# First pair of tiles done plainly, and sums of weights queued behind the layer norm, in the block-product feed-forward parts

## The chip, the cores and the metric

The kernel runs on one core of one Trainium2 chip. The metric is the time of one execution on the device in microseconds; a median of several runs stands for a kernel. TensorE (PE) multiplies, VectorE (DVE) and ScalarE (ACT) do the elementwise work and read products from PSUM, GpSimd (POOL) does some elementwise work in SBUF, and SyncE (SP) issues the transfers.

## What is computed

One step of two hybrid encoder layers over 656 tokens (two request groups side by side), model width 1024, feed-forward width 2816, in float32. Cut to what matters here:

```python
for l in range(2):
    x = post_ln(x, 0.5 * swiglu(x, w_gate[l, 0], w_up[l, 0], w_down[l, 0]))
    x = post_ln(x, mix(l, x))                # even layer: S5 + latent attention; odd layer: attention + retention
    x = post_ln(x, 0.5 * swiglu(x, w_gate[l, 1], w_up[l, 1], w_down[l, 1]))
# swiglu(x, g, u, d) = (silu(x @ g) * (x @ u)) @ d;  post_ln(x, f) = layer_norm(ALPHA * x + f)
```

## The kernel before, in words

Activations lie transposed: features on the partitions, in eight tiles of 128, tokens along the free axis. Each float32 operand of a product is split into a high part `h` (rounded by ScalarE, L286) and a low part `l` (the rest, by VectorE or GpSimd, L289), and each product is three matmuls, h·h, h·l and l·h (`mm3`, `bmm`). `Y3` holds the layer norm's result `y`, `X3` its parts `xh` and `xl`. The norm and the down projection take the tokens in two halves, 336 and 320 columns; the block products take two halves of 328 columns (320 in the last call, where 16 tokens have been dropped).

There are four feed-forward parts. The first (`ffn`) is plain. The other three (`bffn`, for `ff` 1, 2 and 3) form the gate and up products by blocks: a pair of weight tiles times two halves of tokens, with two halves of the contraction, is a 2 x 2 block product, done in seven products P1 to P7 of four contraction tiles each (12 matmuls) where the plain way has eight. P1 and P2 use blocks of the first token half as they are, P3 and P5 blocks of the second half, and P6, P7 and P4 use combinations of blocks, which `combos` makes: differences of `y` in VectorE, then split into `abA` and `abB`. The difference for P5 is written over its block of `xh` and `xl`. On the weight side, `bjob` makes sums and differences of quarter tiles in place in the raw buffers and `ws` (L296 and following), and `bform` splits each result into one of eight half slots of the four pair buffers, in rotation.

At the start of a call, the layer norm of the second half of the tokens is still running. So `bjob_a` first does P1 and P2 for the three pairs of tiles of the first part, gate and up (six jobs of 24 matmuls), which need the first half of the tokens alone; it keeps P1's result in `s1`. The rest of these jobs ("lead jobs") are `bjob` with `s1` given: five products of 12 matmuls each. After the first part come six down tiles' worth of contraction (eight output tiles, `down`), then the second part of the feed-forward width and so on (`SPARTS`: 6, 6, 6 and 4 tiles). The first job of a next part (`ahead`) runs before the down projection of a part, and its last two products among the first down tile.

`layer_norm(h)` runs: sum for the mean on TensorE, differences (VectorE), squares (ScalarE), their sums ending in the "fold" (VectorE), the variance matmul, a reciprocal root of one ScalarE and four VectorE operations (`rsqrt`, L876 to L880), and then `scaled`: a multiplication of two tiles at a time (`ffn_lnt`, VectorE), `xh` on ScalarE (L868), `y` on GpSimd (L869), `xl` on VectorE. With `blocks=True` the first four tiles of the second half get only `y`, on ScalarE (L865), since P5's block is overwritten anyway, and `combos` follows at once.

The order of the instructions on each engine is made by a planner from the order of the program and its own estimate of when each is ready; an instruction written later can go first where an earlier one is not ready. `behind(keys)` ties instructions to named ones of the layer norm (kept in `at`): they stay behind these on that engine. `LN_AFTER` holds such keys for the fetches of `bjob_a` by number; `LN_POOL` names the fetches whose low part is made on GpSimd (0 to 3).

Of the kernel before, what the change touches and what calls it, by code (L numbers as in the profile page):

```python
# [45 lines left out]
LN_AFTER = {1: (("sq", 0, 3),), 2: (("sq", 0, 3),), 3: (("xh", 0, 7), ("y", 0, 7)), 4: (("sq", 1, 3), ("fold", 1, 3))}  # L46
LN_FIRST, LN_FIRST_POOL = LN_AFTER, LN_POOL
# [160 lines left out]
class Prog:  # L208
# [299 lines left out]
    def combos(self):  # L508

        V, w = self.nc.vector, self.wid  # L510
        y = self.Y3
        b11, b12, b21, b22 = (y[:, 4 * i:4 * i + 4, self.cols(j)] for i in range(2) for j in range(2))
# [7 lines left out]
        f = self.forms_x = dict(P1=xb(0, 0), P2=xb(1, 0), P3=xb(1, 1), P5=xb(0, 1), P6=form(at, 0), P7=form(at, 1), P4=form(bt, 0))  # L520
        for c in (0, 2):
            s = slice(c, c + 2)

            def tmp(tag):
                return self.t(tag, [128, 2, 336], F32, 2, self.lnr)[:, :, :w]

            def out(p, d):
                self.split(d, f[p][0][:, s], f[p][1][:, s])
# [5 lines left out]
            out("P6", d2)  # L534
            out("P5", d1)
            d3 = tmp("lnsq")
            self.tt(d3, b22[:, s], b12[:, s], ALU.subtract)
            out("P7", d3)
            d4 = tmp("lnsq")
            V.scalar_tensor_tensor(d4, d2, -1.0, b21[:, s], ALU.mult, ALU.subtract)  # L540
            out("P4", d4)
# [16 lines left out]
    def bconsume(self, gu, q, fi, bank, add, sign):  # L558
# [3 lines left out]
        if gu == 0:  # L562
            if q == (0, 0) and add is None:
# [26 lines left out]

    def bjob_a(self, ff, p, gu, i):

        w = self.job_fetch(self.job(self.I["wgu"][ff, 2 * p, gu], None, None), i, LN_AFTER, LN_POOL)
# [9 lines left out]
    def bjob(self, ff, p, gu, f0, s1=None):  # L603
# [36 lines left out]
        self.tt(s3, a11, a21, ALU.add)  # L640
        self.tt(a21, a21, a22, ALU.add)
        self.tt(a11, a21, a11, ALU.add)
# [19 lines left out]
        self.tt(a12, a11, a12, ALU.add)  # L662
# [5 lines left out]
    def bffn(self, ff, ln_idx, last=False, blocks=False):  # L668
# [46 lines left out]
        for pi, (f0, f1) in enumerate(SPARTS):  # L715
            todo = [(p, gu) for p in range(f0 // 2, f1 // 2) for gu in range(2)]
# [5 lines left out]
            if pi < nparts - 1:  # L722
# [4 lines left out]
                jobs = [down(pi, m) for m in range(8)]  # L727
                for m, j in enumerate(jobs):
# [11 lines left out]
        halves = deque(x[:, :, k:k + 4] for x in self.pairs for k in (0, 4))  # L740
        full, self.pairs = self.pairs, halves
# [14 lines left out]
        self.layer_norm(0, ln_idx, 4.0, last, blocks)  # L756
# [3 lines left out]
        self.layer_norm(1, ln_idx, 4.0, last, blocks)  # L760
        self.pairs = full
# [28 lines left out]
    def mix_out(self, name, ln_idx, h, tick=None, first=True):  # L790

        jobs = [self.out_job(name, m, first) for m in range(8)]
        self.dense_half(jobs, h, {7: lambda: self.layer_norm(h, ln_idx, 1.0, False, True)}, tick)
# [15 lines left out]
    def layer_norm(self, h, idx, epsmul, last, blocks=False):  # L809
# [29 lines left out]
        else:  # L839
            self.scaled(h, idx, last, rs, blocks and h == 1)  # L840
            if blocks and h == 1:
                self.combos()

    def scaled(self, h, idx, last, rs, blocks=False):
# [3 lines left out]
        for m in range(8):  # L848
# [15 lines left out]
            elif blocks and m < 4:  # L864
                at["y", h, m] = nc.scalar.activation(y[:, m], tm, AF.Identity, scale=g[:, m:m + 1], bias=b[:, m:m + 1])  # L865
# [395 lines left out]
    def even_mix(self):  # L1261
# [346 lines left out]
        for hp in range(4):  # L1608
# [4 lines left out]
            for j in range(2):  # L1613
# [18 lines left out]
                   {(h, 7): lambda h=h: self.layer_norm(h, 1, 1.0, False, True) for h in range(2)}, 7)  # L1632
# [488 lines left out]
    def run(self):  # L2121
        tc, nc = self.tc, self.nc
        with tc.tile_pool(name="ps", bufs=1, space=PSUM) as pp, tc.tile_pool(name="dr", bufs=1, space=DRAM) as self.dp:
# [14 lines left out]
            self.bffn(1, 2, blocks=True)  # L2138
# [81 lines left out]
```

## Time and profile before

| | |
|---|---|
| median of 3 runs | 2769.68 us (2768.63 to 2773.45) |
| the profiled execution | 2772.9 us |
| its span, first to last instruction | 2771.1 us |
| mean granted TensorE clock | 0.951 of full speed |
| busy: PE, PEld, DVE, ACT, POOL | 2627.8, 2461.8, 1607.6, 1064.4, 440.4 us |
| matmuls | 17048 |
| moved by the transfers | 243.05 MB |

The profiled execution is 1.8 us longer than its span and 3.2 us longer than the median. A "busy" time is the time in which the engine had at least one instruction running; the busy times of two instructions of one engine overlap a little, since the next starts before the one before has ended. In a timeline a row merges neighbouring instructions of one kind; in brackets stands the engine's idle time before the row and what ended it, and a row without brackets followed without a pause. The granted clock is 1 at 2.4 GHz and 0.5 at 1.2 GHz.

### The profile page before, as it was taken

To read this page: it belongs to the slowest core of one execution; us is meant where nothing else is said; L and a number is where in the kernel's file an instruction comes from. 1 tells how busy PE (TensorE), PEld (TensorE's weight loads), DVE (VectorE), ACT (ScalarE), POOL (GpSimd) and SP (SyncE) were. 2 spreads that over 40 slices of the span, in tenths; PEclk is the share of its full clock that TensorE was granted. 3 is DMA by queue.
4 is the path that set the end of the run, shared out by engine and by line. 5 is a ranking of instruction groups with operands and counts; after the bars stand their busy time and mean duration, and the time that the engine had idled before them with its cause. 6 is when DMAs were issued, how large, how long until landed. Compare 5 with 4: busy or idle time off the path is not lost.

```text
span 2771.1 us, 42830 instructions
## 1 busy us (share of the span) xinstructions
PE 2627.8 (95%) x17048; PEld 2461.8 (89%) x17048; DVE 1607.6 (58%) x2940; ACT 1064.4 (38%) x2010; POOL 440.4 (16%) x557
## 2 busy tenths in 40 slices
PE   9999999999998799999889999989979997999997
PEld 8999999886677799999789999968748996999996
DVE  8343333663436957565895665674323468765756
ACT  3222222434434535343443533343423435443533
POOL 1233311551114000000400000052110023000002
PEclk9999999967998899999989999979979988999998
DMA  4223322342112222222222223222162232322221
GB/s 154 94 87 106 99 93 69 115 126 77 56 41 93 90 84 78 84 80 74 91 79 83 80 81 92 58 64 72 50 204 94 78 126 76 107 77 77 79 86 58
DMA packets 100586, 243.05 MB, mean 88 GB/s; under 512 B 14609, under 2 KB 33186, under 8 KB 100386
## 3 DMA queue, kind: packets, MB, share of 16 engines
q1 hardware_dynamic: 93858, 219.01, 25.2%
q0 software_dynamic: 6528, 21.30, 2.5%
q8 instruction: 134, 2.20, 0.3%
q14 instruction: 66, 0.54, 0.1%
HBM read 221.92 MB, written 17.14 MB: 86 GB/s over the span
## 4 chain that ended last, share of the span: by engine, by line
PE 88%; DVE 6%; ACT 2%; issue 2%; DMA 1%; POOL 1%; SPq 0%; DVEq 0%; ACTq 0%; POOLq 0%
PE psum L267 58%; PE psum L549 27%; PE psum L270 2%; DVE ffn_lnt L296 1%; POOL keep_y L869 1%; DVE ffn_lnva L296 1%; DVE ffn_sg L296 1%; DVE keep_x L289 1%; DVE ring_pair L289 1%; ACT ring_pair L286 1%; DVE keep_y L296 0%; DMA even_in_raw<-uv 0%; DVE ring_raw L296 0%; DVE abA L289 0%; DMA ring_raw<-wdn 0%
## 5 line engine op out<-in xcount | busy, mean ns | idle before, releaser
L286 ACT ACTIVATE ring_pair<-ring_raw 128x512 fp32r<-128x512 f32 (+3 forms) x607 | 448.7, 742 | 824.6 <-PE psum L267 498.6
L267 PE MATMUL psum<-keep_x,ring_pair 128*128 128x320 f32 (+2 forms) x4272 | 700.6, 322 | 31.1 <-ACT ring_pair L286 7.6
L267 PEld LDWEIGHTS psum<-keep_x,ring_pair 128*128 128x128 f32 (+1 forms) x4272 | 657.6, 192 | 54.8 <-DVE keep_x L289 13.0
L289 DVE TENSOR_TENSOR ring_pair<-ring_raw,ring_pair 128x512 fp32r<-128x512 f32 (+3 forms) x587 | 485.1, 829 | 333.7 <-ACT ring_pair L286 321.8
L267 PE MATMUL psum<-hid_hid,ring_pair 128*128 128x320 f32 (+1 forms) x4224 | 650.5, 313 | 2.9 <-DVE ffn_lnt L296 2.3
L267 PEld LDWEIGHTS psum<-hid_hid,ring_pair 128*128 128x128 f32 x4224 | 636.2, 188 | 6.3 <-ACT ring_pair L286 3.4
L549 PE MATMUL psum<-keep_x,ring_pair 128*128 128x328 f32 (+1 forms) x3168 | 526.1, 318 | 46.0 <-ACT keep_x L286 25.9
L549 PEld LDWEIGHTS psum<-keep_x,ring_pair 128*128 128x128 f32 x3168 | 493.3, 193 | 55.0 <-ACT keep_x L286 26.7
L549 PE MATMUL psum<-abA,ring_pair 128*128 128x328 f32 (+1 forms) x1584 | 262.0, 313 | 1.2 <-ACT abA L286 0.7
L549 PEld LDWEIGHTS psum<-abA,ring_pair 128*128 128x128 f32 x1584 | 243.7, 190 | 2.8 <-DVE abA L289 1.3
L296 DVE TENSOR_TENSOR keep_y<-keep_y,psum 128x320 f32<-128x320 f32 (+3 forms) x256 | 138.6, 554 | 173.8 <-PE psum L267 173.4
L296 POOL TENSOR_TENSOR str_s<-keep_y 128x320 f32<-128x320 f32 (+1 forms) x12 | 13.3, 1110 | 1033.9 <-DVE keep_y L296 950.9
L549 PE MATMUL psum<-abB,ring_pair 128*128 128x328 f32 (+1 forms) x792 | 130.4, 311 | 0.0
L549 PEld LDWEIGHTS psum<-abB,ring_pair 128*128 128x128 f32 x792 | 120.8, 188 | 0.2
L869 POOL TENSOR_SCALAR keep_y<-ffn_lnt,keep_cst 128x320 f32<-128x320 f32 (+1 forms) x68 | 78.6, 1167 | 95.9 <-DVE ffn_lnt L296 95.9
L296 DVE TENSOR_TENSOR ring_raw<-ring_raw 128x512 f32<-128x512 f32 x132 | 90.4, 685 | 0.4
L296 DVE TENSOR_TENSOR hid_ws<-ring_raw,ring_raw 128x512 f32<-128x512 f32 x66 | 45.6, 691 | 56.4 <-DMA ring_raw<-wgu 56.1
L286 ACT ACTIVATE hid_hid<-ffn_lnsq 128x328 fp32r<-128x328 f32 (+1 forms) x123 | 57.9, 471 | 52.0 <-DVE ffn_lnsq L296 27.6
L296 POOL TENSOR_TENSOR str_s<-str_s,keep_y 128x320 f32<-128x320 f32 (+1 forms) x60 | 63.5, 1058 | 46.3 <-DVE keep_y L296 26.0
L289 DVE TENSOR_TENSOR hid_hid<-ffn_lnsq,hid_hid 128x328 fp32r<-128x328 f32 (+1 forms) x123 | 60.5, 493 | 17.3 <-ACT hid_hid L286 16.9
L273 POOL MEMSET abA<- 128x16 f32 (+4 forms) x10 | 2.1, 225 | 415.7 <-PE psum L549 388.8
L289 DVE TENSOR_TENSOR keep_x<-keep_y,keep_x 128x320 fp32r<-128x320 f32 (+3 forms) x77 | 55.7, 740 | 16.4 <-POOL keep_y L869 13.1
(437 smaller groups left out, 2671.7 us busy)
## 6 DMA issues: line engine op xcount, KB each, us to landing
ring_raw<-wgu SPq DMA_DIRECT2D x194, 512.0 KB
ring_raw<-wdn SPq DMA_DIRECT2D x88, 384.0 KB
ring_raw<-oin SPq DMA_DIRECT2D x24, 512.0 KB
fox_sample_fvc<-fvn SPq DMA_DIRECT2D x32, 256.0 KB
ring_raw<-oout SPq DMA_DIRECT2D x16, 512.0 KB
ring_raw<-wdn SPq DMA_DIRECT2D x24, 256.0 KB
fox_sample_fkc<-fkt SPq DMA_DIRECT2D x24, 256.0 KB
ring_raw<-wdn SPq DMA_DIRECT2D x16, 320.0 KB
```

Source lines behind the costliest of these rows:

```text
L267: return self.nc.tensor.matmul(out, lhsT, rhs, start=start, stop=stop)
L270: self.nc.tensor.transpose(out, in_, ident)
L273: return self.nc.gpsimd.memset(ap, v)
L286: return self.nc.scalar.activation(out, in_, AF.Copy, scale=scale)
L289: return (eng or self.nc.vector).tensor_tensor(out, a, b_r.bitcast(F32), ALU.subtract)
L296: return (eng or self.nc.vector).tensor_tensor(out, a, b, op)
L549: self.nc.tensor.matmul(ps, a, x, start=start and i + n == 0, stop=i == 3 and n == 2, skip_group_check=not start)
L869: at["y", h, m] = nc.gpsimd.tensor_scalar(y[:, m], tm, g[:, m:m + 1], b[:, m:m + 1], ALU.mult, ALU.add)
```

## The change

In each `bffn` call the first pair of tiles of the first part isn't done by blocks. P1 and P2 come first for the other two pairs (four jobs). Then four whole tiles (gate and up of the two tiles) are fetched and kept in the four pair buffers; each is multiplied by the first half of the tokens (24 matmuls a tile, `classic(0, i)`), then `combos` is written, then the same four tiles by the second half (`classic(1, i)`). The second half of the tokens therefore needs `xh` and `xl` of all eight tiles, and the special case `blocks` in the layer norm goes away: all eight `y` come from GpSimd. The differences for P5, which overwrite that block, move into `rest`, behind the plain products, and their first step is computed again there. The lead jobs are four instead of six.

Sums of weights (`wsum`) and the low parts of forms (`bform`) are put behind `xl` of the second half's last tile. A fetch number 5 gets the same keys as number 4. The forms rotate by a counter, and the down projections take the pair buffers in an order that begins after the slot that the running job uses last.

```diff
+LN_BLOCKS = {**LN_AFTER, 5: LN_AFTER[4]}
...
+        def rest():
+            ds = [tmp("lnt") for _ in range(2)]
+            for d, s in zip(ds, (slice(0, 2), slice(2, 4))):
+                self.tt(d, b11[:, s], b12[:, s], ALU.subtract)
+            for d, s in zip(ds, (slice(0, 2), slice(2, 4))):
+                out("P5", d, s)
+        return rest
+
+    def cjob(self, w, j, consume):
+        ps = self.ps("mm")[:, :self.wid]
+        xh, xl = (x[:, :, self.cols(j)] for x in self.X3)
+        for i in range(8):
+            self.mm3(ps, w[:, 0, i], w[:, 1, i], xh[:, i], xl[:, i], i == 0, i == 7)
+        consume(ps)
...
     def bform(self, src):
-        f = self.forms[0]
-        self.forms.rotate(-1)
-        self.split(src, f[:, 0], f[:, 1])
+        f = self.forms[self.nf % 8]
+        self.nf += 1
+        with self.behind(("xl", 1, 7)):
+            self.split(src, f[:, 0], f[:, 1])
         return f
+    def wsum(self, out, a, b):
+        with self.behind(("xl", 1, 7)):
+            self.tt(out, a, b, ALU.add)
...
     def bffn(self, ff, ln_idx, last=False):
-        for p in range(f0 // 2, f1 // 2):
+        self.bx()
+        for p in range(f0 // 2 + 1, f1 // 2):
             for gu in range(2):
                 s1[p, gu] = self.bjob_a(ff, p, gu, n)
                 n += 1
-        self.forms = deque(x[:, :, k:k + 4] for x in self.pairs for k in (0, 4))
+        order = [(gu, r) for gu in range(2) for r in range(2)]
+        def classic(j, i):
+            gu, r = order[i]
+            self.cjob(cw[i], j, lambda ps: self.bconsume(gu, (r, j), 0, ps, None, 1, True))
+        for i, (gu, r) in enumerate(order):
+            cw.append(self.bweights(ff, f0 + r, gu, n + i))
+            classic(0, i)
+        rest = self.combos()
+        for i in range(4):
+            classic(1, i)
+            self.pairs.append(cw[i])
+        rest()
+        slots = list(self.pairs)
+        self.forms, self.nf = [x[:, :, k:k + 4] for x in slots for k in (0, 4)], 0
...
-            todo = [(p, gu) for p in range(f0 // 2, f1 // 2) for gu in range(2)]
+            todo = [(p, gu) for p in range(f0 // 2 + (pi == 0), f1 // 2) for gu in range(2)]
...
+                a = (self.nf + 1) % 8 // 2 + 1
+                self.pairs = deque(slots[(a + i) % 4] for i in range(4))
...
-        halves = deque(x[:, :, k:k + 4] for x in self.pairs for k in (0, 4))
-        full, self.pairs = self.pairs, halves
+        self.pairs = deque(self.forms[(self.nf + 2 + i) % 8] for i in range(8))
...
-            elif blocks and m < 4:
-                at["y", h, m] = nc.scalar.activation(y[:, m], tm, AF.Identity, scale=g[:, m:m + 1], bias=b[:, m:m + 1])
```

## Rows read from the trace of the kernel before

**Rows 1.** Page, part 1: busy us (share of the span) and instructions.
```profile
PE 2627.8 (95%) x17048; PEld 2461.8 (89%) x17048; DVE 1607.6 (58%) x2940; ACT 1064.4 (38%) x2010; POOL 440.4 (16%) x557
```

**Rows 2.** Windows: length, busy (count) of PE, PEld, DVE, ACT, POOL, clock, DMA, GB/s.
```profile
882.80:910.80 28.00, 26.09 (x148) 24.90 (x146) 26.49 (x41) 20.59 (x34) 10.28 (x9) 0.88 0.24 77
910.80:936.00 25.20, 11.15 (x48) 9.55 (x48) 24.09 (x37) 13.74 (x24) 6.35 (x4) 0.66 0.08 23
936.00:983.00 47.00, 46.95 (x311) 46.81 (x312) 42.45 (x82) 22.50 (x43) 0.00 (x0) 1.00 0.33 107
```

**Rows 3.** Timeline, PE, head 1: start, us, line, operands, count, idle before and releaser.
```profile
882.80 7.29 PE L549 MATMUL psum<-keep_x,ring_pair 128*128 128x328 f32 x36
...
900.05 0.70 PE L267 MATMUL psum<-ffn_lnva,keep_cst 128*128 128x320 f32 x2
900.35 10.30 PE L549 MATMUL psum<-keep_x,ring_pair 128*128 128x328 f32 x66
922.12 0.92 PE L549 MATMUL psum<-keep_x,ring_pair 128*128 128x328 f32 x2 [11.46 <-ACT keep_x L286]
...
936.05 5.64 PE L549 MATMUL psum<-abA,ring_pair 128*128 128x328 f32 x36 [0.15 <-ACT ring_pair L286]
```

**Rows 4.** Timeline, PE, a border between two parts of the first call.
```profile
1120.22 38.01 PE L267 MATMUL psum<-hid_hid,ring_pair 128*128 128x336 f32 x252
1158.07 9.18 PE L549 MATMUL psum<-keep_x,ring_pair 128*128 128x328 f32 x60
```

**Rows 5.** Timeline, PE, head 2.
```profile
1354.13 10.44 PE L549 MATMUL psum<-keep_x,ring_pair 128*128 128x328 f32 x45 [0.61 <-ACT keep_x L868]
...
1377.94 3.85 PE L549 MATMUL psum<-keep_x,ring_pair 128*128 128x328 f32 x24 [0.97 <-ACT str_s L597]
1394.56 0.92 PE L549 MATMUL psum<-keep_x,ring_pair 128*128 128x328 f32 x2 [12.77 <-ACT keep_x L286]
...
1405.97 7.29 PE L549 MATMUL psum<-abA,ring_pair 128*128 128x328 f32 x46 [0.19 <-DVE abA L289]
```

**Rows 6.** Timeline, PE, head 3.
```profile
2291.51 0.46 PE L549 MATMUL psum<-keep_x,ring_pair 128*128 128x320 f32 x2
...
2308.34 2.03 PE L549 MATMUL psum<-keep_x,ring_pair 128*128 128x320 f32 x12 [0.63 <-ACT str_s L597]
...
2315.24 1.44 PE L267 MATMUL psum<-ffn_lnva,keep_cst 128*128 128x320 f32 x2 [4.01 <-DVE ffn_lnva L296]
...
2345.29 8.70 PE L549 MATMUL psum<-abA,ring_pair 128*128 128x320 f32 x53
```

**Rows 7.** Timeline, DVE, head 1, from the fold to the normalising multiplication.
```profile
897.40 0.49 DVE L296 TENSOR_TENSOR ffn_lnva<-ffn_lnva 128x320 f32<-128x320 f32 x1
...
902.50 0.49 DVE L296 TENSOR_TENSOR ffn_sg<-ffn_sg 128x320 f32<-128x320 f32 x1 [0.30 <-ACT ffn_sg L876]
...
908.36 0.69 DVE L289 TENSOR_TENSOR ring_pair<-ring_raw,ring_pair 128x512 fp32r<-128x512 f32 x1
908.96 0.49 DVE L296 TENSOR_TENSOR ffn_sg<-ffn_sg,ffn_sg 128x320 f32<-128x320 f32 x1
...
910.37 1.56 DVE L296 TENSOR_TENSOR ffn_lnt<-keep_y,ffn_sg 128x640 f32<-128x640 f32 x2
```

**Rows 8.** Groups by form, DVE, head 1 and its leads: busy us, mean ns of one.
```profile
L289 DVE TENSOR_TENSOR ring_pair<-ring_raw,ring_pair 128x1024 fp32r<-128x1024 f32 x2 | 2.4, 1222 | 0.0
L289 DVE TENSOR_TENSOR keep_x<-ffn_lnt,keep_x 128x656 fp32r<-128x656 f32 x2 | 1.7, 830 | 0.0
...
L296 DVE TENSOR_TENSOR ffn_lnt<-psum,str_s 128x328 f32<-128x328 f32 x11 | 5.4, 495 | 0.8 <-PE psum L549 0.7
```

**Rows 9.** Timeline, POOL, head 1: `y` of the first half, then of the second.
```profile
882.15 8.56 POOL L869 TENSOR_SCALAR keep_y<-ffn_lnt,keep_cst 128x336 f32<-128x336 f32 x8 [1.37 <-DVE ffn_lnt L296]
...
916.60 6.35 POOL L869 TENSOR_SCALAR keep_y<-ffn_lnt,keep_cst 128x320 f32<-128x320 f32 x4 [23.35 <-DVE ffn_lnt L296]
```

More of the change, by code (lines that the diff above doesn't have):

```diff
@@ L506, in cols, with bx @@
         return slice(a, a + self.wid)
[L508 to L512, printed above, removed]
+    def bx(self):
+        w = self.wid
         at, bt = self.ab("A", F32R), self.ab("B", F32R)
@@ L519, in combos, with tmp, out @@
         xb = lambda i, j: tuple(x[:, 4 * i:4 * i + 4, self.cols(j)] for x in self.X3)
[L520 to L528, printed above, removed]
+        self.forms_x = dict(P1=xb(0, 0), P2=xb(1, 0), P3=xb(1, 1), P5=xb(0, 1), P6=form(at, 0), P7=form(at, 1), P4=form(bt, 0))
+    def combos(self):
+        V, w = self.nc.vector, self.wid
+        y, f = self.Y3, self.forms_x
+        b11, b12, b21, b22 = (y[:, 4 * i:4 * i + 4, self.cols(j)] for i in range(2) for j in range(2))
+        def tmp(tag):
+            return self.t(tag, [128, 2, 336], F32, 2, self.lnr)[:, :, :w]
+        def out(p, d, s):
+            self.split(d, f[p][0][:, s], f[p][1][:, s])
+        for s in (slice(0, 2), slice(2, 4)):
             d1 = tmp("lnt")
@@ L562, in bconsume @@
         if gu == 0:
-            if q == (0, 0) and add is None:
+            if small or (q == (0, 0) and add is None):
                 g = self.t("sg", [128, 336], F32, 2, self.fr[0])[:, :self.wid]
@@ L589, in bconsume, with bweights @@
         self.split(g, hh, hl)
+    def bweights(self, ff, m, gu, i):
+        return self.job_fetch(self.job(self.I["wgu"][ff, m, gu], None, None), i, LN_BLOCKS, LN_POOL)
     def bjob_a(self, ff, p, gu, i):
-        w = self.job_fetch(self.job(self.I["wgu"][ff, 2 * p, gu], None, None), i, LN_AFTER, LN_POOL)
+        w = self.bweights(ff, 2 * p, gu, i)
         ps = self.ps("mm")[:, :self.wid]
@@ L666, in bjob, with bffn @@
         yield
-    def bffn(self, ff, ln_idx, last=False, blocks=False):
+    def bffn(self, ff, ln_idx, last=False):
         nc = self.nc
@@ L755, in bffn @@
                 self.job_run(j, 0, w[m])
-        self.layer_norm(0, ln_idx, 4.0, last, blocks)
+        self.layer_norm(0, ln_idx, 4.0, last)
         for m, j in enumerate(jobs):
@@ L759, in bffn @@
                 self.job_run(j, 1, w[m])
-        self.layer_norm(1, ln_idx, 4.0, last, blocks)
-        self.pairs = full
+        self.layer_norm(1, ln_idx, 4.0, last)
+        self.pairs = deque(slots)
     def job_part(self, j, h, w, a, b, ps=None):
@@ L792, in mix_out @@
         jobs = [self.out_job(name, m, first) for m in range(8)]
-        self.dense_half(jobs, h, {7: lambda: self.layer_norm(h, ln_idx, 1.0, False, True)}, tick)
+        self.dense_half(jobs, h, {7: lambda: self.layer_norm(h, ln_idx, 1.0, False)}, tick)
     def zacc(self, h, m):
@@ L807, in zacc, with layer_norm @@
             self.tt(self.acc[h], self.acc[h], y[:, m], ALU.add, eng)
-    def layer_norm(self, h, idx, epsmul, last, blocks=False):
+    def layer_norm(self, h, idx, epsmul, last):
         nc = self.nc
@@ L839, in layer_norm, with scaled @@
         else:
[L840 to L844, printed above, removed]
+            self.scaled(h, idx, last, rs)
+    def scaled(self, h, idx, last, rs):
         nc = self.nc
@@ L1631, in even_mix @@
         self.dense([self.out_job("ewout", m, first=False) for m in range(8)],
-                   {(h, 7): lambda h=h: self.layer_norm(h, 1, 1.0, False, True) for h in range(2)}, 7)
+                   {(h, 7): lambda h=h: self.layer_norm(h, 1, 1.0, False) for h in range(2)}, 7)
         self.ring_less(1)
@@ L2137, in run @@
             self.even_mix()
-            self.bffn(1, 2, blocks=True)
+            self.bffn(1, 2)
             self.bffn(2, 3)
```

18 lines of the change are left out of this document (9 added, 9 removed).

## The prediction

> **What bounds the kernel now.** I read the page first: TensorE is busy 95% of the span [rows 1], so time can only come from the gaps. The waits of TensorE and its timeline show where they are: the bodies of the feed-forward parts run without a break, for instance straight from 252 matmuls of the down projection into 60 of the next part [rows 4]; the gaps stand at the head of the three `bffn` calls. I call these heads 1, 2 and 3; they start at 882.80, 1354.13 and 2291.51 us [rows 3, 5, 6].
>
> In head 1 TensorE does the first products P1, P2 of six jobs (144 matmuls) from 882.80 to 910.65, the end of the row that starts at 900.35. Then it stands 11.46 us, limps through 48 matmuls, and is steady only from 936.05 [rows 3]. In 910.80 to 936 it did 48 matmuls in 25.2 us, at a mean granted clock of 0.66, so at 1.2 GHz for most of it, after the idle stretch; steady, 311 matmuls take 46.95 us, 0.151 us each [rows 2]. Head 2 is its twin: 12.77 us idle, steady from 1405.97, where 182 of its 504 matmuls are done (the ten rows of products ahead of it) [rows 5]. Head 3 is more broken up: TensorE stands 4.01 us at the variance matmul, then limps to 2345.29, with 175 of 504 done (the 17 rows of products ahead of it) [rows 6].
>
> What ends the long wait is the first P6, whose right side `combos` makes from the normalised second half of the tokens. The windows show VectorE busy 24.09 of 25.2 us there [rows 2], so the head is a VectorE queue, not a latency. The VectorE timeline shows what is in it: the sums and low halves of weights for the first lead jobs stand between the four steps of the reciprocal root. The root starts on VectorE at 902.50 and the normalising multiply only at 910.37 [rows 7]. That is 7.9 us, against some 2 us for its four operations (0.49 each, the first and the last [rows 7], one after the other).
>
> **The change part by part.**
>
> *More matmuls.* A pair of tiles by blocks takes 7 products of 12 matmuls, plainly 2 tiles x 2 halves x 24 = 96. So each gate or up pair costs 12 more, each call 24, and the three calls 72: at 0.151 us that is 10.9 us more TensorE work. This is certain.
>
> *What hides the layer norm.* The work on the first half that needs nothing new rises from 144 matmuls to 96 + 96 = 192, and another 96 (plain, second half) need only `xh`, `xl`, not `combos`. The lead jobs fall from 6 x 60 = 360 matmuls to 240.
> Head 1, if TensorE alone decides: 910.65 + 48 x 0.151 = 917.9, then 14.5 for the second half, 932.4, then 240 x 0.151 = 36.2: the leads end at 968.6. Before: 936.05 + 312 x 0.151 = 983.2. Gain at most 14.6.
> Head 2: 1381.79 + 7.25 + 14.5 + 36.2 = 1439.7; before, the remaining 322 take 48.6 from 1405.97, 1454.6. At most 14.9.
> Head 3 (320 columns; 0.147 us, from 0.151 by the columns): before, the remaining 329 take 48.4 from 2345.29, 2393.7. New: 60 are done by 2308.34, 132 more make 2327.7, one microsecond for weights that stay behind the fold, 14.1, 35.3: 2378. At most 15.6.
> Together at most 45.1 us, the 72 matmuls included.
>
> *Does the second half come in time?* With the sums behind `xl` 1,7 the root costs some 2 us: normalising starts near 904.5 in head 1 (906.8 if two low halves of the plain tiles, 1.22 us each [rows 8], fall into it). All eight `y` now go through GpSimd, before only four. Eight took 8.56 us in the first half's norm, four took 6.35 us in the second half's while VectorE was full [rows 9]: 1.07 to 1.59 us each. So the last `xl` comes at 905.3 + 8.6 + 0.5 = 914.4 at the earliest and 907.6 + 12.7 + 0.5 = 920.8 at the latest. The plain second half starts at 917.9 and reaches its eighth contraction tile at 917.9 + 21 x 0.151 = 921.1: hidden at either end. If that cover were gone, each us later would cost one.
>
> What the Trainium skill says here speaks against this step: SBUF — State Buffer, section "SBUF: two separate sides", has VectorE operations with two SBUF inputs and GpSimd operations exclude each other for a whole instruction. The trace agrees in direction, since the same operation averages 1.59 instead of 1.07 us beside a busy VectorE [rows 9].
>
> *VectorE, the real question.* Its busy time in head 1 and its leads, 882.8 to 983, is 26.49 + 24.09 + 42.45 = 93.0 of 100.2 us, 93% [rows 2]. Operations on 512 elements start 0.60 apart (908.36, 908.96 [rows 7]); from the means of the longer and shorter ones [rows 8] I take 0.09 off likewise: 0.41 for 328, 0.75 for 656, 1.13 for 1024.
> - Two lead jobs gone: 18 sums and low halves x 0.60 = 10.8, 16 operations on products x 0.41 = 6.6.
> - P1, P2 of that pair gone: 0.8.
> - Fetches whose low half is on VectorE, two before, four now: +2.3.
> - Plain up tiles, 4 x 2 x 0.41: +3.3.
> - `rest` forms d1 again, 2 x 0.75: +1.5. Four more `xl`: +2.0.
>
> Net -9.1, so 83.9 us. In 85.8 us (TensorE alone) VectorE would have to be busy 98%; at the 93% it showed, the stage takes 90.2 us and ends at 973.0, a gain of 10.2; at the 90% of the steady lead stretch (42.45 of 47 [rows 2]) 93.2 us, a gain of 7.2. Part of what is late at the end can slide into the next part, whose full jobs ask less of VectorE. I take the middle between 14.6 and 10.2: 12.4 for head 1 and likewise for head 2. Head 3 has the largest ceiling but the more ragged queue; I take 12 there. Sum 36.8 us; ends 3 x 7.2 = 22 and 45.
>
> *Stalls that move.* Next late after the norm is VectorE's `combos`: 14 operations x 0.75 = 10.5 us from about 915, interleaved with the plain up tiles, so done near 927; then the sums of the first lead job. P6 is wanted at 932.4. P5 (`rest`) can be written only when the plain second half has read that block, 12 matmuls before its end, and is wanted 12 matmuls after: 3.6 us for two high and two low halves, about 2.3. Nothing else waits on VectorE in order meanwhile except the products' consumers, and TensorE has five banks.
>
> *Queues.* The four plain tiles bring 4 x 512 KB in place of the two of the first P1, P2 pair and the four of its lead jobs, so SP issues fewer transfers; windows in the heads moved 77 and 23 GB/s where the lead stretch moved 107 [rows 2], so I cost them at 0. Bound: one late tile, 1.0 us of high half plus 1.22 of low half, per head, 0 to 7 in all. The four fetches on GpSimd stay. The plain tiles hold all four pairs until their second half is done; the forms of the first job need the first three of them, freed 3.6 us apart before 932.4: 0.
>
> *Slots at part borders.* The new count puts the first form of each following part into the second half of the slot that the last down tile reads. Its split (0.63 + 0.69) can start only when that tile is done; P2's 12 matmuls (1.8 us), whose slot is free, can go first. Before, the borders show no idle [rows 4]. Bounds 0 to 9 x 1.3 = 12 us; I take 0, being nearest to those rows.
>
> **The rivals.**
> 1. *TensorE alone decides.* VectorE runs on in the next part's slack. For it: 58% overall [rows 1]. Against: 98% in the stage. 2772.9 - 45 = 2728 profiled, 2725 as a median.
> 2. *VectorE decides, with the longer GpSimd chain against it.* At 90% busy, or with four more `y` that each stop VectorE for 1.07 us (4.3 per head off 12.3, about 8 left), the gain is 22 to 24: 2747. With late tiles or the borders' 12 us on top, 2758. For it: rows 9 and the full queue. The rule of SBUF — State Buffer in the Trainium skill, cited above, would make this one.
> 3. *The change doesn't do what it says.* The order is a planner's. If it fills the root's gaps with other VectorE work (`combos` cannot, plain tiles' halves and consumers can), normalising starts near 910 as before, the norm ends at 924, P6 is ready near 940, 7 us late; with clock lost after that gap the gain falls to 3 or less per head: 2762 to 2770.
> 4. *Slower: the variance matmul queues behind the plain work.* TensorE runs in order. In head 1 that matmul ran among the P1 products; if the planner puts it behind all the plain first-half work, at 917.9 instead of 900, the root starts at 918, the norm ends at 933, the second half starts at 922.5 at GpSimd's pace and ends near 943, P6 comes at 946, and the leads end at 982 plus about 4 us of half clock: 986, 3 per head later than before, 2779. It decides from a norm that ends later than about 930. Against it: the matmul ran within 2.2 us of its fold in head 1 (897.9, 900.05 [rows 3, 7]).
>
> **How the numbers follow.** Chances: forecast 0.50, rival 1 0.14, rival 2 0.20, rival 3 0.09, rival 4 0.07. Forecast: profiled 2772.9 - 36.8 = 2736.1. That execution stands 3.2 us above the median of 2769.7, so the median to expect is 2733. Forecast and rivals 1 and 2 hold 0.84, from 2725 less some luck in the norm's earlier start to 2758: 2718 to 2758. A measurement can tell about 0.2%, 5.5 us, from no change: faster by more than that 0.50 + 0.14 + 0.20 + 0.03 of rival 3 = 0.87, same 0.06, slower 0.07.
>
> **What would show it.** In the changed kernel's trace: no weight sums between the root's four steps; the wait of over 11 us before the first P6 gone in heads 1 and 2; granted clock near full from the first plain tile to the leads; leads of head 1 ending 10 to 15 us earlier; VectorE at 95% or more up to there. Wrong if a wait as long stands before the plain second half (rival 4) or spread through the lead jobs on VectorE's low halves (rival 2), or if idle time appears at part borders.

## The result, and the profile after

| | before | after |
|---|---|---|
| median | 2769.15 us (2760.81 to 2773.45, 4 runs) | 2737.73 us (2733.14 to 2744.64, 4 runs) |
| ratio | | 0.9892 [0.986, 0.9925] |
| profiled span | 2771.1 us | 2738.4 us |
| mean granted clock | 0.951 | 0.961 |

The forecast was 2733.0 us, in a range of 2718 to 2758. The profiled spans differ by 32.7 us, where the sum had 36.8.

Part 1 of the page of the changed kernel, to be read beside [rows 1]: 72 matmuls more and 60 VectorE operations fewer, as counted; the share of TensorE is one point higher.

```profile
PE 2619.5 (96%) x17120; PEld 2457.2 (90%) x17120; DVE 1579.5 (58%) x2880; ACT 1050.0 (38%) x1980; POOL 456.2 (17%) x569
```

*Where the time came from.* I measure a head from its first P1 to the last product of its lead jobs (head 3 from the end of the products ahead of it, because in the kernel before two P1 matmuls ran ahead of a wait of 4.0 us that both kernels have).

| us | before | after | gain | forecast |
|---|---|---|---|---|
| head 1 | 100.5 | 91.5 | 9.0 | 12.4 |
| head 2 | 100.7 | 92.3 | 8.4 | 12.4 |
| head 3 | 102.9 | 93.1 | 9.8 | 12 |
| end of head 1 to first P1 of head 2 | 370.8 | 370.8 | 0 | 0 |

So 27.2 of the 32.7 us lie in the heads. Another 2.5 us lie ahead of head 1 (its first P1 came at 882.8, now at 880.3), 2.7 us between the leads of head 2 and the end of the products ahead of head 3, and 0.3 us behind head 3. The runs below show that these can't be told from differences between executions: the stretch ahead of head 1 has the same code in all kernels and ended between 871.7 and 882.9 us, and the one ahead of head 3 took 837.2 and 827.9 us in two kernels with the same code there (the first difference kept, and computed again).

Windows of the changed kernel: head 1 from its first P1 to the end of the plain products, the plain stretch in it that no wait interrupts, the first lead job and what follows it, the steady leads; then heads 1 and 2 as wholes (columns as in [rows 2]).

```profile
880.30:928.60 48.30, 46.81 (x292) 45.03 (x291) 44.02 (x67) 32.28 (x53) 21.29 (x17) 0.97 0.17 56
902.90:928.60 25.70, 25.64 (x171) 25.37 (x170) 23.87 (x39) 16.23 (x28) 10.72 (x8) 1.00 0.08 26
928.60:944.70 16.10, 12.03 (x63) 10.24 (x62) 16.07 (x29) 6.50 (x12) 0.00 (x0) 0.89 0.30 98
944.70:971.80 27.10, 27.10 (x182) 27.10 (x181) 24.93 (x48) 13.96 (x28) 0.00 (x0) 1.00 0.36 104
...
880.30:971.80 91.50, 85.94 (x533) 82.37 (x532) 85.02 (x141) 52.74 (x90) 21.29 (x17) 0.96 0.25 77
1342.60:1434.90 92.30, 86.92 (x536) 83.82 (x537) 83.98 (x140) 52.14 (x89) 21.80 (x17) 0.95 0.24 76
```

The stretch that was 25.2 us with 48 matmuls at clock 0.66 is gone. The plain products run at clock 1.00, and end 48.3 us after the first P1, where the prediction had 49.6 (882.8 to 932.4). But the next 16.1 us hold only 63 matmuls, which at the steady rate (27.10 / 182 = 0.149 us) would take 9.4: 6.7 us are lost there, with VectorE busy 16.07 of 16.10: TensorE stands 4.1 us, and is 2.6 us longer over these matmuls, at a mean granted clock of 0.89. That is all that separates head 1 from TensorE alone (forecast at 968.6 - 882.8 = 85.8; less 1.3, plus 6.7, it is 91.2, against 91.5). VectorE's share of the whole is 85.02 / 91.5 = 93% in head 1, as before; in head 2 it is 91%, where it was 92%.

PE's timeline in head 1 shows the limp, a few matmuls at a time with short waits between (columns as in [rows 3]): it follows the plain products and is made of waits for weights' low halves (`ring_pair`), then for the halves of P5 that `rest` makes (`keep_x`), and for VectorE's reading of a product (`ffn_lnt`).

```profile
895.89 0.70 PE L268 MATMUL psum<-ffn_lnva,keep_cst 128*128 128x320 f32 x2
...
902.89 25.89 PE L268 MATMUL psum<-keep_x,ring_pair 128*128 128x328 f32 x169
928.62 0.76 PE L569 MATMUL psum<-abA,ring_pair 128*128 128x328 f32 x4
929.88 1.02 PE L569 MATMUL psum<-abA,ring_pair 128*128 128x328 f32 x5 [0.50 <-DVE ring_pair L290]
931.68 1.02 PE L569 MATMUL psum<-abA,ring_pair 128*128 128x328 f32 x5 [0.79 <-DVE ring_pair L290]
934.38 0.64 PE L569 MATMUL psum<-keep_x,ring_pair 128*128 128x328 f32 x2 [1.68 <-ACT keep_x L287]
...
941.25 2.06 PE L569 MATMUL psum<-abA,ring_pair 128*128 128x328 f32 x12 [0.68 <-DVE ffn_lnt L297]
```

VectorE's timeline in head 1: the root, the last `xl`, and then steps of `combos` (`abA`, `abB`) with sums of weights (`hid_ws`) among them; the low halves of P5 (`keep_x`, 656 wide) come last.

```profile
894.59 0.49 DVE L297 TENSOR_TENSOR ffn_lnva<-ffn_lnva 128x320 f32<-128x320 f32 x1
...
900.66 0.49 DVE L297 TENSOR_TENSOR ffn_sg<-ffn_sg 128x320 f32<-128x320 f32 x1 [0.72 <-ACT ffn_sg L921]
...
902.60 1.56 DVE L297 TENSOR_TENSOR ffn_lnt<-keep_y,ffn_sg 128x640 f32<-128x640 f32 x2
...
914.52 0.88 DVE L290 TENSOR_TENSOR keep_x<-keep_y,keep_x 128x320 fp32r<-128x320 f32 x2
915.32 0.68 DVE L297 TENSOR_TENSOR hid_ws<-ring_raw,ring_raw 128x512 f32<-128x512 f32 x1
...
934.06 0.83 DVE L290 TENSOR_TENSOR abA<-ffn_lnt,abA 128x656 fp32r<-128x656 f32 x1
...
941.11 0.83 DVE L290 TENSOR_TENSOR keep_x<-ffn_lnt,keep_x 128x656 fp32r<-128x656 f32 x1
```

The root takes 1.9 us on VectorE (900.66 to the multiply at 902.60), not 7.9 as in [rows 7]. The last `xl` is done at 915.4, 35.1 us after the first P1. But the second slice of `combos` is split as late as 934 to 937, and P5 at 941.9.

GpSimd's timeline: all eight `y` of the second half, 10.72 / 8 = 1.34 us each, between the 1.07 and 1.59 of [rows 9].

```profile
903.53 10.72 POOL L914 TENSOR_SCALAR keep_y<-ffn_lnt,keep_cst 128x320 f32<-128x320 f32 x8 [12.66 <-DVE ffn_lnt L297]
```

PE's timeline in head 2, in head 3, and at the border of [rows 4]: the twelve-microsecond wait of [rows 5] is a few short ones, the longest 2.85 us, for a low half of `combos`. In head 3 the longest wait lies in the plain products themselves, 2.62 us for a weight. The border is as unbroken as it was.

```profile
1342.62 1.19 PE L569 MATMUL psum<-keep_x,ring_pair 128*128 128x328 f32 x3 [7.29 <-ACT keep_x L913]
...
1398.55 2.80 PE L569 MATMUL psum<-abA,ring_pair 128*128 128x328 f32 x10 [2.85 <-DVE abA L290]
...
2273.11 8.92 PE L569 MATMUL psum<-keep_x,ring_pair 128*128 128x320 f32 x50 [4.00 <-DVE keep_y L831]
...
2289.75 1.85 PE L268 MATMUL psum<-keep_x,ring_pair 128*128 128x320 f32 x4 [2.62 <-ACT ring_pair L287]
```

```profile
1108.72 38.01 PE L268 MATMUL psum<-hid_hid,ring_pair 128*128 128x336 f32 x252
1146.57 9.18 PE L569 MATMUL psum<-keep_x,ring_pair 128*128 128x328 f32 x60
```

### The profile page after: what moved, and what is told of

It reads as the page before. It is cut to its first block, busy times and chain, and to the rows that moved or that the text cites. A ratio compares the mean times of both kernels' runs of the same rounds, so it can differ in the third digit from the quotient of the medians.

```text
span 2738.4 us, 42851 instructions
## 1 busy us (share of the span) xinstructions
PE 2619.5 (96%) x17120; PEld 2457.2 (90%) x17120; DVE 1579.5 (58%) x2880; ACT 1050.0 (38%) x1980; POOL 456.2 (17%) x569
## 4 chain that ended last, share of the span: by engine, by line
PE 85%; DVE 7%; ACT 2%; DMA 2%; POOL 2%; issue 2%; SPq 0%; DVEq 0%; ACTq 0%; POOLq 0%
PE psum L268 58%; PE psum L569 26%; PE psum L271 2%; POOL keep_y L914 2%; DVE ffn_lnt L297 1%; DVE ffn_sg L297 1%; DVE ring_pair L290 1%; DVE keep_x L290 1%; ACT ring_pair L287 1%; DMA fox_sample_fvc<-fvn 0%; DVE keep_y L297 0%; DVE ffn_lnva L297 0%; DVE ring_raw L297 0%; DMA even_in_raw<-uv 0%; DVE abA L290 0%
## 5 line engine op out<-in xcount | busy, mean ns | idle before, releaser
L268 PE MATMUL psum<-keep_x,ring_pair 128*128 128x320 f32 (+3 forms) x4848 | 786.8, 321 | 35.2 <-ACT ring_pair L287 9.7
L268 PEld LDWEIGHTS psum<-keep_x,ring_pair 128*128 128x128 f32 (+1 forms) x4848 | 741.7, 191 | 60.8 <-DVE keep_x L290 16.3
L569 PE MATMUL psum<-keep_x,ring_pair 128*128 128x328 f32 (+1 forms) x2880 | 468.2, 314 | 17.3 <-ACT keep_x L913 7.3
L569 PEld LDWEIGHTS psum<-keep_x,ring_pair 128*128 128x128 f32 x2880 | 441.2, 190 | 22.5 <-ACT keep_x L913 8.0
L569 PE MATMUL psum<-abA,ring_pair 128*128 128x328 f32 (+1 forms) x1440 | 238.9, 314 | 6.1 <-DVE abA L290 2.9
L569 PEld LDWEIGHTS psum<-abA,ring_pair 128*128 128x128 f32 x1440 | 221.1, 190 | 8.5 <-DVE abA L290 3.4
L569 PE MATMUL psum<-abB,ring_pair 128*128 128x328 f32 (+1 forms) x720 | 119.8, 312 | 0.7 <-ACT ffn_lnt L650 0.7
L569 PEld LDWEIGHTS psum<-abB,ring_pair 128*128 128x128 f32 x720 | 110.1, 188 | 1.2 <-ACT ffn_lnt L650 1.2
L914 POOL TENSOR_SCALAR keep_y<-ffn_lnt,keep_cst 128x320 f32<-128x320 f32 (+1 forms) x80 | 92.4, 1167 | 68.9 <-DVE ffn_lnt L297 68.9
L913 ACT ACTIVATE keep_x<-ffn_lnt,keep_cst 128x320 fp32r<-128x320 f32 (+1 forms) x80 | 47.2, 651 | 48.0 <-DVE ffn_lnt L297 47.9
```

Of the source, the lines that this page charges most:

```text
L268: return self.nc.tensor.matmul(out, lhsT, rhs, start=start, stop=stop)
L569: self.nc.tensor.matmul(ps, a, x, start=start and i + n == 0, stop=i == 3 and n == 2, skip_group_check=not start)
L913: at["xh", h, m] = nc.scalar.activation(xh[:, m], tm, AF.Identity, scale=g[:, m:m + 1], bias=b[:, m:m + 1])
L914: at["y", h, m] = nc.gpsimd.tensor_scalar(y[:, m], tm, g[:, m:m + 1], b[:, m:m + 1], ALU.mult, ALU.add)
```

## The experiments

The theory after the result: the plain pair alone brings the gain, by filling the wait for the norm, and what is left of the heads is decided by VectorE's queue between the norm and P5. Rivals: the order of sums behind the norm brings part of it; TensorE decides; the GpSimd chain decides; or buffers do.

The expectations count the three heads together from the last product of the stage before (before 315.4, after 290.0). That count is 11.3 and 13.1 us longer than the table above, by the waits ahead of the first P1: 5.9 us at head 1 in both kernels, 5.4 and 7.3 us at head 2. Each count is of one profiled execution; the two of the changed kernel agree to 0.3 us in each head. No kernel here leaves any part of the computation out.

| kernel | heads, us | median, us | ratio to before on the same chip |
|---|---|---|---|
| sums not tied | 289.7 | 2733.91 | 0.9898 [0.9875, 0.9921] |
| before + ties alone | 314.3 | 2766.14 | 1.0003 [0.9985, 1.0021] |
| before + slots alone | 319.7 | 2770.0 | 1.0019 [1.0003, 1.0035] |
| sums behind `combos` | 292.5 | 2742.06 | 0.9923 [0.99, 0.9947] |
| four low halves on GpSimd | 292.8 | 2742.38 | 0.9912 [0.9891, 0.9933] |
| four `y` on ScalarE | 291.5 | 2742.93 | 0.9915 [0.9892, 0.9939] |
| more VectorE work | 316.9 | 2761.26 | 0.9983 [0.9968, 0.9997] |
| more TensorE work | 291.6 | 2737.9 | 0.9897 [0.9879, 0.9916] |
| first difference kept | 281.8 | 2728.41 | 0.9871 [0.9849, 0.9893] |
| the same, sums not tied | 280.3 | 2726.16 | 0.9852 [0.9826, 0.9877] |
| the changed kernel again | 290.1 | 2740.74 | 0.9905 [0.9882, 0.9929] |
| kept buffers, recomputed | 288.5 | 2734.34 | 0.9878 [0.9851, 0.9905] |

**Parts of the change.** *Sums not tied to the norm:*

```diff
-        with self.behind(("xl", 1, 7)):
-            self.split(src, f[:, 0], f[:, 1])
+        self.split(src, f[:, 0], f[:, 1])
```
(and likewise in `wsum`)

> The changed kernel without the key: sums of weights and low parts of forms are free to stand inside the layer norm again; the plain pair stays. Theory (VectorE's queue decides the head, the plain pair gives the cover): the norm's root is stretched again from 2 to some 8 us, the last xl comes 6 to 9 us later, near the end of the plain second half's first tiles; the total of VectorE's work is unchanged, so only part of that is lost: 2740 to 2750. Rival (the key is what matters): most of the gain goes, 2757 or more. Rival (the key is worth nothing, TensorE's cover alone decides): within 2 us of the changed kernel.

Heads 289.7: the ties are worth nothing, and the theory, which had 2740 to 2750, was wrong. In GpSimd's timeline the norm's end did become longer, with sums between the root's steps again:

```profile
915.02 12.41 POOL L912 TENSOR_SCALAR keep_y<-ffn_lnt,keep_cst 128x320 f32<-128x320 f32 x8 [15.75 <-DVE ffn_lnt L297]
```

It ends 38.6 us after that head's first P1 (888.82), in the changed kernel 33.9 us (914.25 to 880.30). TensorE waited for `xl` 0.66 us in it. The plain products cover the rest, and the three heads together are as long as they were.

*The ties alone, in the kernel before:*

```diff
+        with self.behind(("xl", 1, 7)):
+            self.split(src, f[:, 0], f[:, 1])
...
+    def wsum(self, out, a, b):
+        with self.behind(("xl", 1, 7)):
+            self.tt(out, a, b, ALU.add)
```

> The kernel before with the key alone: six lead jobs, no plain pair, sums and low parts of forms behind the last xl of the second half. Theory: the norm ends some 6 us earlier, but the sums then stand among combos and the leads have to wait for them; VectorE has the same work as before, so within 6 us of before, 2763 to 2775. Rival (the key is what matters): 2750 or less. In the trace the wait before the first P6 should be shorter by some 5 us and the lead jobs broken up instead.

No difference. PE's timeline of this kernel, head 1, shows the wait of [rows 3] in two pieces, now put down to the weights' forms that were held back:

```profile
916.59 1.52 PE L549 MATMUL psum<-keep_x,ring_pair 128*128 128x328 f32 x4 [8.16 <-ACT ring_pair L286]
922.45 0.92 PE L549 MATMUL psum<-abA,ring_pair 128*128 128x328 f32 x2 [4.35 <-ACT ring_pair L286]
```

*The slots alone, in the kernel before:*

```diff
-        f = self.forms[0]
-        self.forms.rotate(-1)
+        f = self.forms[self.nf % 8]
+        self.nf += 1
...
+                a = (self.nf + 1) % 8 // 2 + 1
+                self.pairs = deque(slots[(a + i) % 4] for i in range(4))
```

> The kernel before with the new order of pair buffers for the down projections and the counter for the forms, nothing else. The changed kernel's three heads gained about 26 of the 32.7 us in the trace; some 6 lie elsewhere. If the order of buffers gives them: 2763 or less, with the idle times of 0.8 and 1.5 us in the last parts gone. If they come from the planner's other choices or from differences between executions: within 3 us of before. If the first form behind each border waits for the last down tile: up to 12 us slower.

The ratio lies just above 1, and the median is 4.6 us above that of the kernel before, more than the 3 us of the second case: the slots bring nothing of the gain. The new order shortens the end of a call's last part by some 2 us, in every kernel that has it, and all of it is given back at the next head's first P1, which waits for the norm (5.4 us in the kernel before, 7.3 us here): end of head 1 to first P1 of head 2 is 370.8 us in both. What else makes these heads longer (319.7 us for 315.4) was not looked into.

**What decides the head.** *The first difference of `combos` computed four times* (six VectorE operations more per head, 6 x 0.75 = 4.5 us):

```diff
-            self.tt(d1, b11[:, s], b12[:, s], ALU.subtract)
+            for _ in range(4):
+                self.tt(d1, b11[:, s], b12[:, s], ALU.subtract)
```

> The changed kernel with the first difference of combos computed four times instead of once: 6 more VectorE operations of 0.75 us, 4.5 us a head, the result the same. From the first P1 to the last lead product head 1 took 91.6 us in the changed kernel, VectorE busy 93%. Theory (VectorE's total decides the head): each head 4 to 5 us longer, together 12 to 15 us: 2748 to 2753. Rival (TensorE decides, VectorE has slack): within 4 us of the changed kernel, 2734 to 2742.

The three heads grew by 26.9 us for 13.5 us of work, two for one where the theory had 12 to 15 us, and nearly the whole gain was gone. PE's timeline, then windows of the same stretch (columns as in [rows 2]):

```profile
931.07 1.77 PE L570 MATMUL psum<-abA,ring_pair 128*128 128x328 f32 x10 [3.02 <-DVE abA L290]
939.86 0.92 PE L570 MATMUL psum<-abA,ring_pair 128*128 128x328 f32 x2 [7.02 <-ACT abA L287]
```

```profile
900.80:927.60 26.80, 26.80 (x181) 26.80 (x180) 24.98 (x40) 15.79 (x27) 10.75 (x8) 1.00 0.09 32
...
931.07:939.86 8.79, 1.77 (x11) 1.51 (x11) 8.79 (x15) 1.23 (x2) 0.00 (x0) 0.81 0.19 65
939.86:950.00 10.14, 8.95 (x41) 8.47 (x42) 7.64 (x12) 3.45 (x5) 0.00 (x0) 0.66 0.15 52
950.00:978.40 28.40, 28.40 (x191) 28.40 (x190) 25.57 (x50) 14.65 (x28) 0.00 (x0) 1.00 0.34 101
```

The three heads as wholes in this kernel, then head 3 of the changed one, whose heads 1 and 2 stand above:

```profile
878.20:978.40 100.20, 87.37 (x534) 85.33 (x533) 90.53 (x149) 52.98 (x90) 21.05 (x17) 0.91 0.22 71
1349.15:1449.13 99.98, 88.65 (x536) 85.74 (x537) 89.35 (x148) 53.08 (x90) 21.00 (x17) 0.90 0.23 71
2277.16:2380.80 103.64, 88.61 (x536) 85.20 (x537) 88.72 (x141) 50.31 (x84) 22.27 (x17) 0.92 0.23 74
```

```profile
2269.11:2362.17 93.06, 84.22 (x537) 81.33 (x537) 83.78 (x136) 49.74 (x84) 22.31 (x17) 0.96 0.26 83
```

VectorE is busy without a break while TensorE stands. After the 7.02 us wait TensorE is busy 8.95 us with 41 matmuls, at a mean granted clock of 0.66 between its levels of 1.2 and 2.4 GHz, where 0.149 us each would be 6.1. The slower clock is the smaller part of the second microsecond, since the changed kernel has such a stretch too: over the heads TensorE's busy time grew by 1.4, 1.7 and 4.4 us, 7.5 of the 26.9. The other 19.4 us are waits of TensorE. VectorE's busy time grew by 15.8 us in all, and it stands longer too, in head 1 once for a product that TensorE brings late (VectorE's timeline):

```profile
950.71 0.50 DVE L297 TENSOR_TENSOR ffn_lnt<-psum,str_s 128x328 f32<-128x328 f32 x1 [3.21 <-PE psum L570]
```

So the two engines wait for each other in turn, and VectorE's share fell, to 90% in head 1. The added work stands in `combos` itself, ahead of P6; no run added work elsewhere in VectorE's queue, so whether its place matters is not shown.

*One plain tile multiplied twice* (24 matmuls more per head, 10.9 us in all):

```diff
+        for _ in range(again):
             for i in range(8):
                 self.mm3(ps, ...)
...
+            self.cjob(..., 2 if (j, i) == (1, 0) else 1)
```

> The changed kernel with the first tile of the plain second half multiplied twice: 24 more matmuls a head, 3.6 us, 10.9 us in all. Theory (VectorE's total decides the head, and TensorE waits for it in the first lead job): the added work takes the place of that wait, so most of it is free: 0 to 4 us, 2736 to 2742. Rival (TensorE decides): all of it shows, 2747 to 2750. If both are near their limit in turn, about half: 2743.

Heads 1 and 2 were 1.2 and 2.4 us shorter with 3.6 us more work in each: VectorE gains the time that TensorE fills, and most of the limp is gone (PE's timeline, head 1):

```profile
906.16 29.19 PE L268 MATMUL psum<-keep_x,ring_pair 128*128 128x328 f32 x193
935.19 1.95 PE L570 MATMUL psum<-abA,ring_pair 128*128 128x328 f32 x12
```

Head 3 was 5.1 us longer, 3.5 us of work and a wait of 1.73 us for a weight in the plain products that the changed kernel doesn't have: there the rival's case holds. Together 1.6 us for 10.9.

*Sums behind all of `combos`* (its second pass through the loop sets the key last) instead of the last `xl`:

```diff
-            out("P4", d4, s)
+            self.hi(f["P4"][0][:, s], d4)
+            self.at["cb", 0, 0] = self.sub(f["P4"][1][:, s], d4, f["P4"][0][:, s])
...
-        with self.behind(("xl", 1, 7)):
+        with self.behind(("cb", 0, 0)):
```

> The changed kernel with the key moved: sums and low parts of forms stand behind the last low part of combos instead of behind the last xl. In the changed kernel's trace the second half of combos ends some 20 us after the last xl, since sums for two lead jobs stand between. Theory (VectorE's total decides, order is second): within 4 us of the changed kernel, 2734 to 2742, with the wait before P5, P7 and P4 shorter but one before P6's weights in its place. Rival (the order on VectorE costs the limp in the first lead job, about 5 us a head): 2722 to 2730.

Heads 292.5: `combos` is ready earlier, the weights' forms later. VectorE's timeline in head 1, then PE's:

```profile
923.34 0.83 DVE L290 TENSOR_TENSOR abB<-ffn_lnsq,abB 128x656 fp32r<-128x656 f32 x1
```

```profile
928.04 0.42 PE L570 MATMUL psum<-keep_x,ring_pair 128*128 128x328 f32 x1 [1.92 <-ACT ring_pair L287]
```

The last low half of `combos` is done at 924.2, 46.6 us after that head's first P1 (877.6), where the changed kernel took 57; but TensorE now waits for a form ahead of the first lead product, and head 1 took 91.8 us against 91.5. So this other order of the same work brings nothing.

**GpSimd.** *The low halves for P7 and P4 on GpSimd* (four operations of 0.75 us off VectorE per head):

```diff
-            out("P7", d3, s)
+            out("P7", d3, s, self.nc.gpsimd)
...
-            out("P4", d4, s)
+            out("P4", d4, s, self.nc.gpsimd)
```

> The changed kernel with the low parts of P7's and P4's combinations made on GpSimd, which is idle after the norm: 4 operations of 0.75 us a head leave VectorE, 3 us. If VectorE's total decides and GpSimd doesn't hinder it: 2 to 3 us a head, 2729 to 2733. If a GpSimd operation with two inputs stops VectorE while it runs (in the kernel before a VectorE pair of 128x336 took 3.08 us beside the GpSimd low part of a fetch): no gain, or up to 4 us lost: 2737 to 2742.

No gain: heads 292.8. GpSimd's timeline, then the groups of VectorE's operations by form in head 1 of this kernel, then of the changed one:

```profile
918.54 1.84 POOL L290 TENSOR_TENSOR abA<-ffn_lnsq,abA 128x656 fp32r<-128x656 f32 x1
925.10 4.05 POOL L290 TENSOR_TENSOR abA<-ffn_lnsq,abA 128x656 fp32r<-128x656 f32 x1 [4.73 <-ACT abA L287]
```

```profile
L297 DVE TENSOR_TENSOR ring_raw<-ring_raw,ring_raw 128x512 f32<-128x512 f32 x5 | 4.7, 963 | 0.0
L290 DVE TENSOR_TENSOR hid_hid<-ffn_sg,hid_hid 128x328 fp32r<-128x328 f32 x6 | 4.2, 695 | 0.0
```

```profile
L297 DVE TENSOR_TENSOR ring_raw<-ring_raw,ring_raw 128x512 f32<-128x512 f32 x5 | 3.4, 683 | 0.0
L290 DVE TENSOR_TENSOR hid_hid<-ffn_sg,hid_hid 128x328 fp32r<-128x328 f32 x6 | 3.2, 535 | 0.0
```

The work took 1.84 to 4.05 us an operation on GpSimd, and some of the operations that stayed on VectorE became longer (963 for 683 ns, 695 for 535): VectorE was busy 86.62 us in that head, with four operations fewer, against 85.02. The rule cited in the prediction (the Trainium skill, SBUF — State Buffer, section "SBUF: two separate sides") says that a VectorE operation with two SBUF inputs and a GpSimd operation that reads SBUF exclude each other, the one that starts second standing until the first is done; the trace agrees in these longer operations. For the eight `y` of the change the prediction feared a loss by it that can't be seen: they took 1.34 us each, and the next run, with four of them off GpSimd, has VectorE busy 84.73 us in head 1, hardly less than 85.02.

*Four of the eight `y` on ScalarE:*

```diff
+                if h == 1 and m < 4:
+                    at["y", h, m] = nc.scalar.activation(y[:, m], tm, AF.Identity, scale=..., bias=...)
```

> The changed kernel with the first four y of the second half back on ScalarE (with xh kept as well), so that GpSimd has four instead of eight. Theory (the norm's end is hidden by the plain work): no effect, within 3 us of the changed kernel, 2734 to 2741, although the last xl comes some 4 us earlier. Rival (GpSimd's longer chain or its hold on VectorE costs the head, 1 us for each operation): 3 to 4 us a head less, 2726 to 2729.

291.5, no gain. The last `xl` was done 34.6 us after the first P1, hardly sooner than 35.1, where the expectation had some 4 us, so this run moved the chain too little to price it. But four operations fewer on GpSimd made no head shorter by the 1 us each of the rival. That a longer chain costs nothing is shown by the first experiment, where it ended 4.7 us later.

**Towards a better kernel.** *The first difference of `combos` kept for P5*, in a buffer of the norm for one slice and two `s1` buffers for the other, instead of being computed again:

```diff
+        kept = []
...
+            if not kept:
+                parts = [(self.t("lnva", ...), s)]
+            else:
+                parts = [(self.t("s1", ...), k) for k in (2, 3)]
+            kept += parts
...
-            ds = [tmp("lnt") for _ in range(2)]
-            for d, s in zip(ds, (slice(0, 2), slice(2, 4))):
-                self.tt(d, b11[:, s], b12[:, s], ALU.subtract)
...
+            for d, s in kept:
                 out("P5", d, s)
```

> The changed kernel with the first difference of combos kept (in the norm's variance buffer and two s1 buffers) instead of made again in rest: 1.3 us less VectorE work a head, and the two lnt buffers serve the second differences alone, so the second half of combos needn't wait for them. The three heads, from the last matmul of the stage before to the last lead product, took 97.4, 99.6 and 93.1 us in the changed kernel. If VectorE's work decides as in the run with 6 operations more (8 to 10 us a head for 4.5): 2 to 3 us less a head, 2729 to 2733. If only the total counts: 1 us less a head, 2734 to 2736. If neither: as the changed kernel, 2737.

*The same, sums not tied:*

> The same with the key on sums and low parts taken away. The key alone and its removal moved nothing so far (2766 against 2765; 2734 against 2738), so: within 3 us of the run with the difference kept. If the key helps once combos is shorter: 3 us or more slower than that.

*The changed kernel itself again, on the same chip:*

> The changed kernel itself once more, on the same chip as the two before it: 2734 to 2742, heads within 1 us of the first profile. It shows how far one execution of the same program stands from another outside the heads: the first P1 came at 880.3 in its first profile and between 877.6 and 888.8 in the variants, none of which differs ahead of it.

Heads 281.8 and 280.3, against 290.1 for the changed kernel (which so repeats to 0.1 us; its median was 2740.74). The last one is the fastest of all: 2726.16 us (2721.06 to 2728.63), 14.6 us below the changed kernel on that chip, 9.8 of them in the heads. Whether the ties are kept or not is not told apart here either: the two ratios overlap.

*The same buffers, but the difference computed again*, to tell the work from the freed `lnt` buffers:

```diff
             for d, s in kept:
+                self.tt(d, b11[:, s], b12[:, s], ALU.subtract)
+            for d, s in kept:
                 out("P5", d, s)
```

> The kernel with the kept difference, but rest makes that difference again into the same buffers: VectorE's work is that of the changed kernel (1.6 us a head more than with the difference kept), while the second differences still have the two lnt buffers to themselves. With the difference kept the three heads took 281.8 us together, in the changed kernel 290.0. If VectorE's total made the 8 us: heads together 287 or more. If the two buffers, for which the second half of combos waited, made them: 283 or less. Between: both.

Heads 288.5: 6.7 us more than with the difference kept, while VectorE's busy time in the three heads grew by 4.5 us. That leaves 1.6 us of the 8.2 for the buffers. PE's timeline of head 1, first with the difference kept, then with it computed again:

```profile
932.58 0.76 PE L572 MATMUL psum<-abA,ring_pair 128*128 128x328 f32 x4
...
934.93 1.77 PE L572 MATMUL psum<-abA,ring_pair 128*128 128x328 f32 x10 [1.44 <-DVE ring_pair L290]
```

```profile
932.56 0.56 PE L574 MATMUL psum<-abA,ring_pair 128*128 128x328 f32 x2
...
936.03 0.64 PE L574 MATMUL psum<-keep_x,ring_pair 128*128 128x328 f32 x1 [2.41 <-DVE ffn_sg L297]
```

The medians of these two were taken on different chips and their ratios overlap, so this rests on the heads, one execution of each. Head by head this kernel stands 0.3 and 3.0 us below the changed one and 1.9 us above it, so how work and buffers share the 8.2 us is not settled; that the work is most of it is what the sum says.

## Why the prediction was right, and where it was off

- *The plain pair hides the norm:* right. The 11 to 13 us waits [rows 3, 5] are gone, the clock over the plain products is 1.00, and the last `xl` at 35.1 us after the first P1 lies in the forecast's 31.6 to 38.0. The cover is wide: the norm's end could be 4.7 us later (sums not tied) at no cost. With ties and slots worth nothing, the plain pair brings the gain; which part of it is the cover and which the saved VectorE work was not separated.
- *Sums behind the norm shorten the root to 2 us:* right as a fact, 1.9 us, but it carries nothing of the gain, as both experiments with the ties show. The prediction priced both edits as one mechanism; in the kernel before, too, the ties alone were worth nothing.
- *VectorE's ledger:* 83.9 us forecast, 85.0 measured in head 1. The rule that it stays at 93% gave 10.2 us for head 1; the measured share is 93% there and the gain 9.0. It is no rule of the stage, though: the share is 91 and 90% in heads 2 and 3, and in the other kernels it went from 86% (more VectorE work, head 3) to 95% (first difference kept, sums not tied, head 2).
- *The step that was mis-sized* is the one after: "the middle between 14.6 and 10.2", 12.4 for heads 1 and 2, with the reason that what is late can slide into the next part. It did not slide: TensorE waits inside the first lead job. 9.0, 8.4 and 9.8 us in place of 12.4, 12.4 and 12 are 27.2 instead of 36.8. The lower bounds by VectorE (10.2 and 7.2) enclose the measured ones for heads 1 and 2.
- *"Done near 927, P6 is wanted at 932.4":* this is where the missing time is. Counted from the first P1, the second slice of `combos` was to be split by 44 us and came at 54 to 57; sums for two lead jobs stand among its steps, and `rest` recomputes its difference behind them. The stall that moved is 6.7 us there. The order is not the fault: with all sums behind `combos`, as the prediction had them, it was done by 46.6 us and head 1 was no shorter. What the prediction had wrong is that VectorE gets through `combos` and the forms of the first lead jobs before TensorE wants them.
- *"Beside a busy VectorE"* was misread from [rows 9]: VectorE was busy 7.59 of the 8.56 us of the eight `y` and 5.40 of the 6.35 us of the four, so these rows don't show what a busy VectorE costs GpSimd. As bounds 1.07 and 1.59 held (1.34).
- *Borders 0, queues 0:* right. The slots won some 2 us in the last part and lost them at the next head.
- *Rivals:* TensorE alone (rival 1) falls with the two kernels that add work, except in head 3. VectorE deciding (rival 2) was the right mechanism for what remained, but through its own queue and not through GpSimd's chain. Sums filling the root's gaps (rival 3) did happen without the ties, and cost nothing. The variance matmul (rival 4) stayed among the P1 products, at 895.89, 0.8 us after its fold had ended.
- The remaining 5.5 us of the profiled gain lie where the code is the same and executions differ by as much. That the median came within 5 us of the forecast, with heads 9.6 us short of it, is luck to that extent. What in the stretch ahead of head 1 and in the one ahead of head 3 varies by some 10 us from run to run was not looked into and stays open.

## What to carry to other kernels

Fill a wait with work that needs less of the engine that is full, not merely with work that can start: the plain pair also took VectorE operations away (85.0 us in head 1 for 93.4), and when 5.5 us of work were put back there, head 1 was as long as before (100.1 us for 100.5) with the same plain work. Where an engine is busy 93% of a stage, size an edit by that share rather than by an average with a bound in which another engine is alone, but expect less than it gives: it fell in two heads of three here, and when work was added. An operation computed again to save a buffer is dear in such a stage; look for any buffer that is idle just then.

## What the hardware showed that was not expected

VectorE work added in the full stretch cost two for one (26.9 us for 13.5): 19.4 us of it are waits of TensorE, and 7.5 the same matmuls taking longer, as in the 10 us after a 7 us wait, at a mean granted clock of 0.66. And moving four operations from VectorE to GpSimd did not lower VectorE's busy time: it rose from 85.02 to 86.62 us in head 1.
